# A mixture-of-experts layer: the first expert's turn on unsplit weights with 64 slots, and three more weight blocks loaded ahead

## Chip, cores and metric

The kernel runs on one core of one Trainium2 chip. The metric is device time in microseconds (us), the median of several executions; lower is better. Names of engines: PE (TensorE), DVE (VectorE), ACT (ScalarE), POOL (GpSimd), SP (SyncE, which issues nearly all loads of weights).

## What is computed

A trunk of two layers over 256 tokens of width 1024, all in float32. Each layer has a token mixer and a channel mixer; the channel mixer of the second layer is a mixture of 8 experts of which every token takes two:

```python
logits = h @ router
top_v, top_i = lax.top_k(logits, 2)
wts = softmax(top_v)
combine = sum(one_hot(top_i, 8) * wts)
for e in range(8):
    y = y + combine[..., e:e+1] * ((silu(h @ w1[e]) * (h @ w3[e])) @ w2[e])
```

with `w1`, `w3` of 1024 x 3584 and `w2` of 3584 x 1024. The router, worked out on the reference's own inputs, sends 60, 58, 49, 84, 77, 59, 69 and 56 tokens to experts 0 to 7.

## The kernel before

The change lies in `moe`, the second layer's experts, which is the last part of the program. All eight experts' weights pass once through the core as 336 blocks of 1024 KB, 42 of each expert: seven groups j of 512 hidden columns, in each two blocks of `w1`, two of `w3` and two of `w2`. The `w2` blocks of a group come after the `w1` and `w3` blocks of the next group, so that the first block of the second turn is the 41st of the stream, and that of the third turn the 83rd.

**Turns.** The experts are taken in eight turns. Expert 0 always has turn 0, so that its loads need no routing; the seven others are ordered by their number of tokens (`RANK`) and read by a register that SP loads once (`loads`, L1312). Expert 0 and the three fullest others take the "big" way, the four others the "small" one (`SMALL`), in turns that alternate: big, small, big, small and so on.

- A big turn has 128 slots. Each weight piece of 1024 columns is split into a rounded part `hi` (ACT, L1187) and the rest `lo` (DVE, L1188), and every tile of it costs three matmuls of 512 columns: L1408, L1409, L1410 for `w1` and `w3` (`up`), L1426 to L1428 for `w2` (`down`).
- A small turn has 64 slots (`CAP`). The float32 weights go to PE as they landed, as two half-width matmuls side by side (L1404 in `up`, L1423 in `down`), with no work on ACT and DVE for the weights.

The tokens of a turn are gathered by one-hot matmuls (`slots_of`, `gather`, L1377) into `xs` (small) or `xh`, `xl` (big); one gather serves a pair of turns (`GROUPS`). The results go back by `back` and `scatter`. If the count of tokens of an expert exceeds its slots (`excess`), a second part (`spill`) runs all experts again, twice.

**Loads.** `fetch` keeps the blocks on their way. At the start it issues as many as there are names in `FIRST`: 18, namely the places of two tiles that are needed only later (`acts`, `late`), fifteen `raw` buffers and `y`. After that only the `raw` names go round. SP issues loads strictly in order; a load waits for the release of its buffer, and for the load eight before it to have landed.

```python
live, blocks, expert = [], [], [0]
slots = list(FIRST)
```

A block's buffer is released in a big turn by DVE, when `lo` of its second piece is written, in a small turn by PE, after the block's last matmul. `hi` and `lo` have three buffers of 1024 columns each (`SPLIT_MOE`), six places of 512 KB. The order of instructions on PE, DVE, ACT and SP is that of the code: `pieces` yields one weight piece after another, and at each a clock ticks, on which the small steps hang (`after`, `SORT`, `BACK`).

Of the kernel before, what the change touches and what calls it, by code (L numbers as in the profile page):

```python
# [9 lines left out]
F32 = mybir.dt.float32  # L10
F32R = mybir.dt.float32r
# [3 lines left out]
ALU = mybir.AluOpType  # L15
# [3 lines left out]
P = 128  # L19
T = 256  # L20
D = 1024
KC = 8
# [5 lines left out]
NE = 8  # L28
# [29 lines left out]
NPRE = len(PRE)  # L58


RANK = [7, 0, 4, 1, 5, 2, 6, 3]
SMALL = [False, True] * 4
CAP = 64
NSMALL = sum(SMALL)
GROUPS = [(None, 0), (1, 2), (3, 4), (5, 6), (7, None)]


def constants():
# [14 lines left out]
    put("keyc", np.broadcast_to(np.array([1e6, 1, 2, 3, 4, 5, 6, 7])[None, :], (P, 8)))  # L83
    put("seq", np.broadcast_to(np.array(RANK)[None, :], (P, 8)))
    gmask = ((s <= t) & (i[:, None] // 64 == i[None, :] // 64)).astype(np.int32)
# [350 lines left out]
WOUT = ((2, 'BT'), (3, 'TT'))  # L436
MOE_BUFS = 15
PLACES = [f"raw{i}" for i in range(6)] + ["acts", "late"] + [f"raw{i}" for i in range(6, MOE_BUFS)]
FIRST = ["acts", "late"] + [f"raw{i}" for i in (6, 7, 8, 4, 5, 12, 13, 14, 9, 10, 11, 2, 3, 1, 0)] + ["y"]
PACE = (13, 9, 28)  # L440
PACED_FROM = 8
ARAW_BUFS = 2
# [4 lines left out]
SPLIT_MOE = 3  # L447
SUB = 1024
# [685 lines left out]
def moe(k, l, out):  # L1134
    tc, nc, A = k.tc, k.nc, k.A
    ctx = ExitStack()
    dp = ctx.enter_context(tc.tile_pool(name="moe", bufs=1, reuse_waits="tile"))
    sp = ctx.enter_context(tc.tile_pool(name="moew", bufs=1, reuse_waits="tile"))
# [12 lines left out]
    todo = [o + (h,) for o in order for h in range(2)]  # L1151
    live, blocks, expert = [], [], [0]

    once = {n: sp.tile([P, 2048], F32, name=n) for n in PLACES}
    once["y"] = dp.tile([P, 2048], F32, name="y")
    slots = list(FIRST)

# [18 lines left out]
    def prepare(eng=nc.vector):  # L1176

        block = blocks[0]
        w, at, _ = block
        q = len(part)  # L1180
        s = slice(q * SUB, (q + 1) * SUB)
        last = q == 2048 // SUB - 1
        if SMALL[at[0]]:
            ready.append((w[:, s], None, at + (q,), block if last else None))
        else:
            hi, lo = [sp.tile([P, SUB], F32R, name=n, bufs=SPLIT_MOE) for n in ("hi", "lo")]
            nc.scalar.activation(hi, w[:, s], AF.Copy)  # L1187
            eng.tensor_tensor(lo, w[:, s], hi.bitcast(F32), ALU.subtract)  # L1188
            ready.append((hi, lo, at + (q,), None))
        part.append(q)  # L1190
        if last:
            part.clear()
            blocks.pop(0)
            if not SMALL[at[0]]:
                done(block)
# [3 lines left out]
    def parts(n, kind=F32):  # L1199

        if n not in held:
            held[n] = sp.tile([P, 4, 512], kind, name=n)
        return held[n]

    turns = [0, 0]

    def room():
        turns[0] += 1
# [3 lines left out]
    ready = []  # L1212
    fetch(len(FIRST))

# [9 lines left out]
    n8, key, rank, more, idx = [S8[:, i] for i in range(5)]  # L1224
# [66 lines left out]
    def sort():  # L1291

        by = lambda a: a[:, None, :].to_broadcast([P, NE, NE])
        of = lambda a: a[:, :, None].to_broadcast([P, NE, NE])
        p, w = perm[:, 0], perm[:, 1]

        def ranks():
            nc.vector.scalar_tensor_tensor(key, n8, 8.0, k.k("keyc"), ALU.mult, ALU.add)
            nc.vector.tensor_tensor(w, of(key), by(key), ALU.is_gt)
            nc.vector.tensor_reduce(rank, w, AX.X, ALU.add)  # L1300
            nc.vector.tensor_tensor(p, by(rank), of(k.k("seq")), ALU.is_equal)
            nc.vector.tensor_tensor(w, p, by(iota[:, :NE]), ALU.mult)
            nc.vector.tensor_reduce(idx, w, AX.X, ALU.add)
            nc.vector.tensor_copy(idxi, idx)

        def turned(src, dst):
            for tt in range(2):
                nc.vector.tensor_tensor(w, p, by(src[:, tt]), ALU.mult)
                nc.vector.tensor_reduce(dst[:, tt], w, AX.X, ALU.add)

        def loads():
            _, v = nc.values_load_multi_w_load_instructions(idxi[0:1, 1:NE], engines=[mybir.EngineType.SP], min_val=0,  # L1312
                                                            max_val=NE - 1)
            expert.extend(v)

        def excess():
            nc.vector.tensor_scalar(more, rank, NSMALL - 0.5, float(P - CAP), ALU.is_le, ALU.mult)
            nc.vector.tensor_tensor(n8, n8, more, ALU.add)
            nc.vector.tensor_reduce(cnt, n8, AX.X, ALU.max)
            nc.vector.tensor_copy(cnti, cnt)  # L1320

        return [ranks, loads, lambda: turned(posm, posm_s), lambda: turned(comb, comb_s), excess]
# [13 lines left out]
    def slots_of(g):  # L1336

        Pm = dp.tile([P, 2, 2, P], F32R, name="Pm", bufs=2)
        for i, (t, io) in enumerate(zip(GROUPS[g], (iod, iota))):
            if t is not None:  # L1340
# [6 lines left out]
    def back(g, Pm, gs, PT):  # L1347
        pg = k.pg()
        here = [i for i in range(2) if GROUPS[g][i] is not None]
        for i in here:  # L1350
# [12 lines left out]

    def places(g):

        xs = dp.tile([P, KC, CAP], F32, name="xs") if GROUPS[g][0] is not None else None
        xl = [dp.tile([P, KC, P], F32R, name=n) for n in ("xh", "xl")] if GROUPS[g][1] is not None else None
        return xs, xl

# [28 lines left out]
    def up(e, j, b, p, x):  # L1398
        for o, hi, lo in pieces(e, j, b):
            for z in range(SUB // 512):  # L1400
                kc = o + z
                if SMALL[e]:
                    for n in range(2):
# [8 lines left out]
    def down(e, j, py, act):  # L1412
        if j == 0:
            py += [k.pc() for _ in range(1 if SMALL[e] else 2)]
        for o, hi, lo in pieces(e, j, 2):
            for n in range(2):
                for z in range(SUB // 1024):
                    c = o // 2 + z
                    s = slice(z * 1024 + n * 512, z * 1024 + n * 512 + 512)
                    first, last = j == 0 and c == 0, j == NJ - 1 and c == 3  # L1420
                    if SMALL[e]:
                        a = (c % 2) * P + (c // 2) * CAP
# [170 lines left out]
    for _ in range(PRESPLIT):  # L1593
        prepare()
    with tc.manual_schedule(engines=ORDERED | LOADS):
        y = choose()
        idle = k.pj()
        busy(IDLE[0])
        pp = place()
        busy(IDLE[1])  # L1600
        for c in range(3):
            rows_of(c, y)
        rows_of(0, y, True)
        nc.vector.tensor_tensor(posm, posm, pp[:, 0:2 * NE].rearrange("p (a b) -> p a b", a=2), ALU.add)
        new = slots_of(0)
        nc.vector.tensor_copy(n8, pp[:, 2 * NE:3 * NE])
        rows_of(1, y, True)
        rows_of(2, y, True)
        to = places(0)
        for kc in range(KC):  # L1610
            gather(0, new[1], kc, to, k.pj if kc % 4 > 1 else k.pg)
        weigh()
        after(BACK, lambda: back(*new))
        for n, f in enumerate(sort()):
            after(SORT + n, f)
        group = new, to
        for e in range(NE):
            i = 0 if SMALL[e] else 1
            if e and i == 0:
                group = nxt  # L1620
            (_, _, gs, PT), (xs, x2) = group
            for j in range(NJ):
                ph = [k.pj()]
                up(e, j, 0, ph[0], x2 if i else xs)
                act, steps = hidden(e, ph)
                delay = DELAY
                if (e, j) == (NE - 1, NJ - 1):
                    delay, last = LAST, gains()
                after(delay[0], steps[0])
                ph.append(k.pj())  # L1630
                up(e, j, 1, ph[1], x2 if i else xs)
                for d, f in zip(delay[1:], steps[1:]):
                    after(d, f)
                if i == 1 and e < NE - 1:
                    g = e // 2 + 1
                    if j == NJ - 2:
                        new = slots_of(g)
                        after(BACK, lambda: back(*new))
                    if j == NJ - 1:
                        nxt = new, places(g)  # L1640
                        for kc in range(KC):
                            after(kc * 2048 // SUB // 4, lambda kc=kc, g=g, n=nxt: gather(g, n[0][1], kc, n[1]))
                if pend:
                    down(*pend[:4])
                    if pend[4]:
                        for d, f in in_turn(pend[0], *scatter(pend[0], pend[2], *pend[4])):
                            after(d, f)
                if j == 0:
                    py = []
                pend = (e, j, py, act, (gs[:, i:i + 1], PT, i) if j == NJ - 1 else None)  # L1650
        while tasks:
            tick()
        down(*pend[:4])
        banks = iter((k.pg, k.pg, k.pj, k.pj))
        finish(scatter(pend[0], pend[2], *pend[4], lambda: next(banks)()), *last)
# [64 lines left out]
    n = nc.values_load(cnti[0:1, 0:1], min_val=0, max_val=T + P)  # L1720
# [103 lines left out]
```

## Time and profile before

| what | value |
|---|---|
| median of 3 runs | 1780.85 us (1779.85 to 1782.62) |
| the profiled execution | 1777.78 us, of which its span 1776.0 us |
| PE busy | 1703.6 us, 96% of the span |
| DVE, ACT busy | 1161.7 us (65%), 838.2 us (47%) |
| DMA | 520.92 MB, mean 293 GB/s |
| blocks of expert weights | 336 loads, 1024 KB each |

The profile gives, for any stretch, the busy time of each engine, the granted clock of PE (1.00 is 2.4 GHz, 0.50 is 1.2 GHz) and what the DMA engines moved; it lists instructions in order of time, and what each waited for. Busy shares of PE say little alone, since matmuls are pipelined and their ends are modelled.

### The profile page before, as it was taken

What the parts mean: (1) busy time and instruction counts of PE and PEld (TensorE: products, weight loads), DVE (VectorE), ACT (ScalarE), POOL (GpSimd) and SP (SyncE); (2) the same over time, 40 slices, a digit from 0 to 9 for tenths busy, and PEclk for the clock granted to TensorE, in tenths of its full rate; (3) what the DMA queues carried; (4) which work ended last, traced back from release to release, by engine and by line L of the source; (5) the groups of instructions that cost most, each with busy time, mean ns of one, the idle gap of its engine ahead of it and who ended that gap; (6) DMA issues with size and microseconds to landing.
All of it is one profiled execution on the core that took longest, in us unless ns stands there. A gap on an engine that the chain in (4) does not pass through costs nothing.

```text
span 1776.0 us, 30054 instructions
## 1 busy us (share of the span) xinstructions
PE 1703.6 (96%) x11915; PEld 1400.8 (79%) x11915; DVE 1161.7 (65%) x1783; ACT 838.2 (47%) x1214; POOL 50.3 (3%) x100
## 2 busy tenths in 40 slices
PE   7998989989999799999999999999999999999997
PEld 6987879989999688799977875688656876578754
DVE  3789577787876879466669950588407972289611
ACT  3653234454444743244547740477306771267501
POOL 0000010010100000000000000000000000000001
PEclk9999899999999899899989999999999999999999
DMA  9445257687874333225678989999999999999995
GB/s 347 158 165 190 73 182 259 249 287 304 314 267 145 110 129 119 73 96 190 261 307 311 366 314 421 421 421 421 418 420 421 421 421 416 421 421 421 420 421 214
DMA packets 79972, 520.92 MB, mean 293 GB/s; under 512 B 9520, under 2 KB 10160, under 8 KB 22352
## 3 DMA queue, kind: packets, MB, share of 16 engines
q1 hardware_dynamic: 67440, 476.14, 67.7%
q0 software_dynamic: 11232, 40.90, 6.7%
q8 instruction: 95, 1.56, 0.4%
q10 hardware_dynamic: 1152, 1.89, 0.3%
q14 instruction: 53, 0.43, 0.1%
HBM read 517.84 MB, written 1.05 MB: 292 GB/s over the span
## 4 chain that ended last, share of the span: by engine, by line
PE 76%; issue 8%; DMA 7%; DVE 6%; ACT 1%; POOL 0%; SPq 0%; ACTq 0%; POOLq 0%; DVEq 0%
PE pj L1404 11%; PE pj L392 7%; PE pj L393 7%; PE pj L394 7%; PE pc L1423 6%; PE pj L1408 5%; PE pj L1410 5%; PE pj L1409 5%; DMA araw<-wada 4%; PE pc L1426 3%; PE pc L1428 3%; PE pc L1427 3%; DMA raw<-moe 2%; PE pg L1453 1%; DVE lo L369 1%
## 5 line engine op out<-in xcount | busy, mean ns | idle before, releaser
L1188 DVE TENSOR_TENSOR lo<-raw,hi 128x1024 fp32r<-128x1024 f32 x330 | 396.1, 1223 | 85.0 <-ACT hi L1187 77.9
L1187 ACT ACTIVATE hi<-raw 128x1024 fp32r<-128x1024 f32 x330 | 347.5, 1059 | 128.1 <-PE pj L1409 80.0
L367 ACT ACTIVATE hi<-raw 128x1024 fp32r<-128x1024 f32 (+2 forms) x209 | 213.9, 1025 | 280.7 <-PE pj L393 207.6
L369 DVE TENSOR_TENSOR lo<-raw,hi 128x1024 fp32r<-128x1024 f32 (+2 forms) x209 | 246.5, 1181 | 77.5 <-ACT hi L367 73.9
L392 PE MATMUL pj<-hh,hi 128*128 128x256 f32 x992 | 289.9, 292 | 4.8 <-DVE t L418 3.4
L394 PE MATMUL pj<-hh,lo 128*128 128x256 f32 x992 | 285.9, 288 | 1.3 <-DVE lo L369 1.3
L393 PE MATMUL pj<-hl,hi 128*128 128x256 f32 x992 | 286.2, 289 | 0.0
L1404 PE MATMUL pj<-raw,xs 128*64 128x256 f32 x1792 | 201.4, 381 | 0.0
L392 PEld LDWEIGHTS pj<-hh,hi 128*128 128x128 f32 x992 | 191.2, 193 | 12.1 <-issue 4.8
L394 PEld LDWEIGHTS pj<-hh,lo 128*128 128x128 f32 x992 | 191.1, 193 | 2.5 <-DVE lo L369 1.8
L393 PEld LDWEIGHTS pj<-hl,hi 128*128 128x128 f32 x992 | 191.3, 193 | 2.2 <-issue 1.3
L1408 PE MATMUL pj<-hi,xh 128*128 128x512 f32 x448 | 181.3, 405 | 0.5 <-ACT hi L1187 0.5
L1410 PE MATMUL pj<-lo,xh 128*128 128x512 f32 x448 | 178.5, 398 | 2.0 <-DVE lo L1188 1.9
L1409 PE MATMUL pj<-hi,xl 128*128 128x512 f32 x448 | 177.7, 397 | 0.0
L1404 PEld LDWEIGHTS pj<-raw,xs 128*64 128x64 f32 x1792 | 125.8, 137 | 64.9 <-issue 4.7
L1448 DVE TENSOR_TENSOR late<-late,pj 128x512 f32<-128x512 f32 (+1 forms) x56 | 30.8, 550 | 207.6 <-PE pj L1404 201.0
L1410 PEld LDWEIGHTS pj<-lo,xh 128*128 128x128 f32 x448 | 84.5, 189 | 25.7 <-DVE lo L1188 5.4
L1423 PE MATMUL pc<-raw,as 128*64 128x512 f32 x448 | 102.2, 595 | 0.0
L1408 PEld LDWEIGHTS pj<-hi,xh 128*128 128x128 f32 x448 | 84.8, 189 | 21.2 <-ACT hi L1187 1.9
L1409 PEld LDWEIGHTS pj<-hi,xl 128*128 128x128 f32 x448 | 84.7, 189 | 18.7
L256 DVE SCALAR_TENSOR_TENSOR aacc<-araw,csg,aacc 128x1024 f32<-128x1024 f32 x70 | 89.6, 1280 | 8.0 <-DMA araw<-wada 7.5
L1426 PE MATMUL pc<-hi,acts 128*128 128x512 f32 x224 | 88.3, 394 | 0.0
(432 smaller groups left out, 2749.2 us busy)
## 6 DMA issues: line engine op xcount, KB each, us to landing
raw<-moe SPq DMA_DIRECT2D x333, 1024.0 KB, 18.6
raw<-win SPq DMA_DIRECT2D x43, 1024.0 KB, 5.0
araw<-wada POOLq DMA_DIRECT2D x78, 512.0 KB, 5.3
raw<-f SPq DMA_DIRECT2D x33, 1024.0 KB, 7.3
raw<-wv SPq DMA_DIRECT2D x8, 1024.0 KB, 4.8
raw<-wog SPq DMA_DIRECT2D x8, 1024.0 KB, 5.0
raw<-wad SPq DMA_DIRECT2D x6, 1024.0 KB, 7.1
raw<-wor SPq DMA_DIRECT2D x4, 1024.0 KB, 5.1
```

The lines of the kernel that those rows point to most:

```text
L367: nc.scalar.activation(hi[:, :w], src, AF.Copy)
L369: nc.vector.tensor_tensor(lo[:, :w], src, hi[:, :w].bitcast(F32), ALU.subtract)
L392: nc.tensor.matmul(o, hi[:, s], ah[:, kc, :], start=kc == 0, stop=False)
L393: nc.tensor.matmul(o, hi[:, s], al[:, kc, :], start=False, stop=False)
L394: nc.tensor.matmul(o, lo[:, s], ah[:, kc, :], start=False, stop=kc == nk - 1)
L1187: nc.scalar.activation(hi, w[:, s], AF.Copy)
L1188: eng.tensor_tensor(lo, w[:, s], hi.bitcast(F32), ALU.subtract)
L1404: nc.tensor.matmul(p[64 * n:64 * n + 64, :T], x[:, kc], hi[:, z * 512 + n * T:z * 512 + n * T + T], start=kc == 0, stop=kc == KC - 1)
L1408: nc.tensor.matmul(p, x[0][:, kc], hi[:, s], start=kc == 0, stop=False)
L1409: nc.tensor.matmul(p, x[1][:, kc], hi[:, s], start=False, stop=False)
L1410: nc.tensor.matmul(p, x[0][:, kc], lo[:, s], start=False, stop=kc == KC - 1)
L1423: nc.tensor.matmul(py[0][64 * n:64 * n + 64], act[:, a:a + CAP], hi[:, s], start=first, stop=last)
```

## The change

Turn 0 becomes a small one. `SMALL` is now small, small, big, small, big, small, big, small: expert 0 has 64 slots and unsplit weights, and the three fullest of the others stay big. `GROUPS[0]` gathers only `xs`, 64 columns; the `xs` of turn 1, gathered during turn 0, lies in the fourth quarter of `late`. The test for too many tokens adapts to the new table. The pairs `hi` and `lo` become one tile of 2048 columns, `hl0` to `hl2`; since these are not needed before turn 2, they carry the 19th to 21st block at the start.

```diff
-SMALL = [False, True] * 4
+SMALL = [True] + [True, False] * 3 + [True]
 CAP = 64
-NSMALL = sum(SMALL)
-GROUPS = [(None, 0), (1, 2), (3, 4), (5, 6), (7, None)]
+GROUPS = [(0, None), (1, 2), (3, 4), (5, 6), (7, None)]
...
-FIRST = ["acts", "late"] + [f"raw{i}" for i in (6, 7, 8, 4, 5, 12, 13, 14, 9, 10, 11, 2, 3, 1, 0)] + ["y"]
+FIRST = ["acts", "late"] + [f"raw{i}" for i in (6, 7, 8, 4, 5, 12, 13, 14, 9, 10, 11, 2, 3, 1, 0)] + ["y"] + [
+    f"hl{i}" for i in range(3)]
...
-    once = {n: sp.tile([P, 2048], F32, name=n) for n in PLACES}
+    once = {n: sp.tile([P, 2048], F32, name=n) for n in PLACES + [f"hl{i}" for i in range(SPLIT_MOE)]}
...
-            hi, lo = [sp.tile([P, SUB], F32R, name=n, bufs=SPLIT_MOE) for n in ("hi", "lo")]
+            hl = sp.tile([P, 2 * SUB], F32R, name=f"hl{turns[2] % SPLIT_MOE}")
+            turns[2] += 1
+            hi, lo = hl[:, :SUB], hl[:, SUB:]
...
-            nc.vector.tensor_scalar(more, rank, NSMALL - 0.5, float(P - CAP), ALU.is_le, ALU.mult)
+            nc.vector.tensor_scalar(more, rank, -5.0, None, ALU.add)
+            nc.vector.tensor_tensor(more, more, more, ALU.mult)
+            nc.vector.tensor_scalar(more, more, 2.0, float(P - CAP), ALU.is_ge, ALU.mult)
...
-        xs = dp.tile([P, KC, CAP], F32, name="xs") if GROUPS[g][0] is not None else None
+        xs = None
+        if g == 1:
+            xs = parts("late")[:, 3].rearrange("p (k n) -> p k n", k=KC)
+        elif GROUPS[g][0] is not None:
+            xs = dp.tile([P, KC, CAP], F32, name="xs")
...
-                if i == 1 and e < NE - 1:
+                if (i == 1 or e == 0) and e < NE - 1:
```

On SP, around the first loads of `moe`; DMAHW names stand for the load eight before, DVE and PE for the engine that releases the buffer. Before:

```order
L1163 DMA raw0_9796<-moe 128x2048 [waits DMAHW1_49]
L1163 DMA y_9813<-moe 128x2048 [waits DMAHW2_49]
L1163 DMA raw6_10042<-moe 128x2048 [waits DMAHW3_49,DVE_49]
L1163 DMA raw7_10074<-moe 128x2048 [waits DMAHW4_49,DVE_49]
L1312 TENSOR_LOAD idxi_9838 [waits DVE_49]
L1312 ISA x14
L1163 DMA raw8_10168<-moe 128x2048 [waits DMAHW5_49,DVE_49]
```

And now:

```order
L1164 DMA raw0_9796<-moe 128x2048 [waits DMAHW1_49]
L1164 DMA y_9816<-moe 128x2048 [waits DMAHW2_49]
L1164 DMA hl0_9813<-moe 128x2048 [waits DMAHW3_49]
L1164 DMA hl1_9814<-moe 128x2048 [waits DMAHW4_49]
L1164 DMA hl2_9815<-moe 128x2048 [waits DMAHW5_49]
L1315 TENSOR_LOAD idxi_9844 [waits DVE_49]
L1315 ISA x14
L1164 DMA raw6_10135<-moe 128x2048 [waits DMAHW6_49,PE_49]
```

Three loads that wait for no compute engine have come in ahead of the register load, and the first load that reuses a buffer stands behind it and waits for PE in place of DVE.

On DVE, at the start of `moe`, where the one-hot tile `Pm` for the first gather is made. Before:

```order
L1604 TENSOR_TENSOR R<-R,pj 128x16
L1188 TENSOR_TENSOR lo<-acts,hi 128x1024 x2
L1343 TENSOR_SCALAR Pm<-cst,R 128x128 x2
L1606 COPY S_9837<-pj 128x8
L1277 SCALAR_TENSOR_TENSOR tl<-pc,rsq,th 128x384
L1188 TENSOR_TENSOR lo<-late,hi 128x1024
```

And now:

```order
L1613 TENSOR_TENSOR R<-R,pj 128x16
L1348 TENSOR_SCALAR Pm<-iod,R 128x128 x2
L1615 COPY S_9843<-pj 128x8
L1280 SCALAR_TENSOR_TENSOR tl<-pc,rsq,th 128x384 x2
L1280 SCALAR_TENSOR_TENSOR tl<-ada,rsq,th 128x256
```

The two `lo` pieces that stood ahead of `Pm` are gone, as are all splits of turn 0.

On ACT, in turn 2, the first that is big in both kernels: the splits of `w1` pieces. Before:

```order
L1187 ACTIVATE hi_11635<-raw13_11474 128x1024 [waits DMAHW5_49,DVE_49,PE_49]
L1187 ACTIVATE hi_11645<-raw13_11474 128x1024 [waits DVE_49,PE_49]
L1187 ACTIVATE hi_11658<-raw14_11488 128x1024 [waits DMAHW6_49,DVE_49,PE_49]
L1187 ACTIVATE hi_11668<-raw14_11488 128x1024 [waits DVE_49,PE_49]
L1445 ACTIVATE late_10025<-pj_11611 128x512
```

And now:

```order
L1190 ACTIVATE hl2_11099<-raw14_10928 128x1024 [waits DMAHW1_49,DVE_49,PE_49]
L1190 ACTIVATE hl0_11104<-raw14_10928 128x1024 [waits DVE_49,PE_49]
L1190 ACTIVATE hl1_11121<-raw9_10934 128x1024 [waits DMAHW2_49,DVE_49,PE_49]
L1485 ACTIVATE ys_11119<-pc_10681,gs_10399 128x512 [waits PE_49]
L1190 ACTIVATE hl2_11131<-raw9_10934 128x1024 [waits DVE_49,PE_49]
```

The order is the same; the target is now a tile that holds the `lo` part too, so that a new `hi` waits for the last matmul that reads either part (the `lo` product) where it waited for the last that reads `hi`, one matmul earlier.

## Rows read from the trace of the kernel before

**Rows 1.** Stretches of 50 us: length, busy of PE, PEld, DVE, ACT, POOL, PEclk, DMA share, GB/s

```profile
900.00:950.00 50.00, 44.50 (x194) 35.14 (x194) 39.71 (x94) 30.77 (x42) 0.00 (x0) 0.90 0.87 357
950.00:1000.00 50.00, 50.00 (x224) 40.72 (x223) 45.35 (x42) 39.54 (x42) 0.00 (x0) 1.00 0.94 358
1000.00:1050.00 50.00, 48.69 (x266) 39.08 (x266) 37.09 (x45) 33.99 (x49) 0.00 (x0) 1.00 0.84 309
1050.00:1100.00 50.00, 50.00 (x366) 29.47 (x364) 10.44 (x18) 6.46 (x13) 0.00 (x0) 1.00 1.01 415
```

**Rows 2.** The same view for the rest of the experts' stage

```profile
1060.00:1750.00 690.00, 686.07 (x4002) 473.51 (x4000) 370.06 (x411) 319.89 (x399) 2.90 (x8) 1.00 1.01 420
...
1752.00:1754.00 2.00, 2.00 (x10) 0.69 (x10) 0.00 (x0) 0.38 (x1) 0.00 (x0) 1.00 0.24 98
```

**Rows 3.** Instructions of PE in order of time: starts of turns, last product

```profile
916.23 0.73 PE L1408 MATMUL pj<-hi,xh 128*128 128x512 f32 x1
...
1044.12 7.13 PE L1404 MATMUL pj<-raw,xs 128*64 128x256 f32 x64
...
1125.32 0.48 PE L1408 MATMUL pj<-hi,xh 128*128 128x512 f32 x1
...
1755.76 2.31 PE L1423 MATMUL pc<-raw,as 128*64 128x512 f32 x10
```

**Rows 4.** What SP's queue waited for from 909 to 1060 us: total, times, longest

```profile
SPq L1163 <- DVE lo L1188: 96.5, 33, 12.8
...
SPq L1312 <- DVE lo L1188: 7.9, 1, 7.9
```

**Rows 5.** SP's loads in order of time after the first seventeen

```profile
909.31 0.33 SPq L1163 DMA_DIRECT2D y<-moe  x1
924.60 0.33 SPq L1163 DMA_DIRECT2D raw<-moe  x1
...
938.07 0.81 SPq L1163 DMA_DIRECT2D raw<-moe  x2
```

**Rows 6.** DMA issues: the 18th block, KB, us from issue to landing

```profile
y<-moe SPq DMA_DIRECT2D x1, 1024.0 KB, 19.9
```

**Rows 7.** DVE and PE in order of time, at the first gather

```profile
906.66 2.35 DVE L1188 TENSOR_TENSOR lo<-acts,hi 128x1024 fp32r<-128x1024 f32 x2
...
909.35 0.49 PE L1377 MATMUL pg<-Pm,th 128*128 128x128 f32 x2 [1.79 <-DVE Pm L1343]
```

**Rows 8.** Stretches of 10 us, columns as in rows 1

```profile
910.00:920.00 10.00, 9.95 (x38) 8.99 (x38) 5.99 (x21) 4.20 (x10) 0.00 (x0) 0.50 1.01 422
920.00:930.00 10.00, 10.00 (x46) 7.84 (x45) 6.05 (x6) 6.98 (x8) 0.00 (x0) 1.00 1.02 422
```

**Rows 9.** PE in turn 7, a small one: four blocks of `up`, two of `down`

```profile
1700.12 7.13 PE L1404 MATMUL pj<-raw,xs 128*64 128x256 f32 x64
...
1707.08 3.60 PE L1423 MATMUL pc<-raw,as 128*64 128x512 f32 x16
```

**Rows 10.** DVE in order of time: the ranks' first and last step

```profile
932.78 0.16 DVE L1298 SCALAR_TENSOR_TENSOR S<-S,cst 128x8 f32<-128x8 f32 x1
...
934.27 0.17 DVE L1304 CAST idxi<-S 128x8 int32<-128x8 f32 x1
```

**Rows 11.** PE's groups from 916 to 1044 us: busy, mean ns, idle before (`tl` has as many)

```profile
L1377 PE MATMUL pg<-Pm,th 128*128 128x192 f32 x16 | 3.2, 283 | 0.6 <-DVE xl L1384 0.6
```

**Rows 12.** ACT, DVE and PE in order of time in turn 2, one piece

```profile
1168.72 1.06 ACT L1187 ACTIVATE hi<-raw 128x1024 fp32r<-128x1024 f32 x1 [0.34 <-PE pj L1409]
...
1169.81 1.23 DVE L1188 TENSOR_TENSOR lo<-raw,hi 128x1024 fp32r<-128x1024 f32 x1 [0.17 <-ACT hi L1187]
...
1171.79 0.39 PE L1409 MATMUL pj<-hi,xl 128*128 128x512 f32 x1
...
1172.02 0.40 PE L1410 MATMUL pj<-lo,xh 128*128 128x512 f32 x1
```

**Rows 13.** DVE in turn 2: a step that stands between the splits

```profile
1176.52 0.68 DVE L1448 TENSOR_TENSOR late<-late,pj 128x512 f32<-128x512 f32 x1
```

More of the change, by code (lines that the diff above doesn't have):

```diff
@@ L1203, in parts @@
         return held[n]
-    turns = [0, 0]
+    turns = [0, 0, 0]
     def room():
```

## The prediction

> **What bounds the kernel now.** I looked first at the stretches of 50 us, not at busy shares: PE is busy for 96% of the span, which would make it the bound and the change a plain saving of PE work. The column of the transfers says something else. From 1060 us on they move 420 GB/s without a break [rows 2]; that is the most that any longer stretch shows, so a block of 1024 KB (1.049 MB) costs 1.049 / 420 = 2.50 us of transfer, however early it is asked for. Before that, the same stream runs at 357, 358, 309 and 415 GB/s [rows 1]. Against 420 that lacks 63 + 62 + 111 + 5 = 241 GB/s in stretches of 50 us, or 241 x 50 / 420 = **28.7 us** of transfer time that is never won back, since the stream is full for all the rest.
>
> Why it lacks is in the waits of SP's queue: from 909 to 1060 us it stood 96.5 us behind `lo` of turn 0, DVE's release of a buffer, and 7.9 us before the register load [rows 4]. The 18th block was issued at 909.31 and landed 19.9 us later, at 929.2; the next loads went out at 924.60 and shortly after, and then none until 938.07 [rows 5, 6], so the queue ran dry after the second of them.
>
> PE has hardly more room. Turn 0 runs from 916.23 to 1044.12 (127.9 us), turn 1 to 1125.32 (81.2 us), and from there to the end of the last product at 1758.07 it takes 632.8 us [rows 3], 686.07 of 690 us busy [rows 2]. The last block lands at about 1753 [rows 2], 5 us before that product ends. So transfers and PE are matched to about 1% in the pairs of turns; what differs is turn 0, where one resource waits for the other.
>
> **The change, part by part.** *Loads.* The rows of SP show three new loads, each waiting only for the load eight before. `y` went out when the tenth block landed (909.31), so the three follow at steps of 2.50: 911.8, 914.3, 916.8, and land at 931.7, 934.2 and 936.7. The next load must go out before some 934 us for the stream to stay full. It now waits for two things. First PE: the third block must be used. PE begins earlier, since `Pm` no longer stands behind 2.35 us of `lo` and the first gather waited for `Pm` [rows 7], and that gather has half the columns. It took 916.23 - 909.35 = 6.9 us [rows 3, 7]; with half of it and the 2.35 us off, turn 0 would start at 910.4, and I take 912; at full clock a small block costs (7.13 + 3.60) / 6 = 1.79 us [rows 9], at half clock 3.58, so three blocks are used at 917 to 923. Second the register load, which follows on the ranks; these stand behind a copy that waits for PE after three blocks, take 1.7 us [rows 10], and the load after them came 938.07 - 934.44 = 3.6 us later [rows 5, 10]: 923 to 929. Either way the queue is still full, with 5 us to spare. After that, blocks are released every 1.8 us by PE and needed every 2.50 us: no load waits for a buffer until turn 2. The stream then has no hole: the 83rd block, the first of turn 2, lands at 929.2 + 65 x 2.50 = 1091.5, and the last, 318 blocks after `y`, at 1724, against some 1753 now. This term is **minus 28.7 us**; between nothing (all waits return in another form) and this value I take nearly all of it, because DVE's release, 96.5 us of the waits, no longer exists before turn 2.
>
> *PE.* Turn 0 now has 40 blocks of 1.79 us (72 us) before the first of turn 1, the gather for turns 1 and 2 of twice 3.2 us [rows 11], and up to 5 us for 10 us at half clock [rows 8]: from 912 to about 996, against 1044.12. Turn 1 adds its 81.2 us: PE would want the 83rd block at 1077 and gets it at 1091.5. So of some 45 us that PE saves, the last 15 are spent waiting, and turn 2 starts with the first split after that block (1.06 us on ACT [rows 12]) at 1092.6: 32.7 us earlier than 1125.32. From there PE needs its 632.8 us again.
>
> *Splits.* In three big turns a new `hi` now waits for the `lo` product. In the piece of [rows 12] ACT starts at 1168.72, `lo` is written by 1171.04 and needed at 1172.02: 0.98 us of room. One matmul later means 1172.02 - 1171.79 = 0.23 us less; a DVE step in between takes 0.68 us [rows 13]. That still fits, by 0.07 us, so a single delay costs nothing; where two meet (scatter, gather, starts of turns) PE may lose 0.23 us each. Bounds: none, and 3 turns x 84 pieces x 0.23 = 58 us if every piece paid. The row is nearest to none; I take 2 us. PE's own sum is then -32.7 + 2 = -30.7; that of the transfers, -28.7, is the smaller gain and decides.
>
> *Small things.* The longer test for too many tokens is two more operations on eight columns, 0.17 us each by the cast of [rows 10], on a DVE that has no splits left in turn 0: nothing. The `xs` of turn 1 in `late` uses a quarter that nothing else reads then: nothing. The tail after the last product is unchanged.
>
> Sum: 28.7 less a little for starts that don't fit exactly, **minus 28 us**. The profiled execution (1777.78) would become 1749.8; the median of the runs stands 3.1 us above it, so I predict **1752.9 us**.
>
> **A cold PE.** Turn 1 has something that this stage never had: PE waiting for weights. It needs 81.2 / 42 = 1.93 us a block there, its transfer 2.50, so that from 996 on it has caught up at about the 57th block (1027 us) and then waits some 0.6 us at each. PE was granted 1.2 GHz from 910 to 920 us, after it had stood for 1.79 us before `Pm`, and 2.4 GHz in the next ten, after work without a break [rows 7, 8]. At 1.2 GHz a small block takes 3.58 us, more than its transfer; PE would fall behind and be busy without a break, which is what brought the clock back. Such a spell loses some 5 us, and only what is missing at the 83rd block counts: a spell just there leaves a gain of 32.7 - 5 - 2 = 26 us. Were the clock low from the 57th block to the 83rd, 26 x 3.58 = 93 us would bring PE there at 1120, and 5 us of gain were left. I count on the row: a PE without a break gets its clock back. The Trainium skill ("TensorE: Matmul & The Clock Gate", section "HAM oscillation — how this bites in real kernels") warns of exactly such a loop, where each tile's work is shorter than the wait for the next weights and the clock drops at every tile; by that rule turn 1 would stay slow, and the sum would be the 5 us. No row here shows waits as short as 0.6 us that come again and again, so whether it holds for them is open.
>
> **Rivals.** (1) *Only the three blocks count.* The refills come as late as before for another reason (the register load, PE's start), and all that is won is 3 x 2.50 = 7.5 us: 1773. For it: 7.9 us of SP's wait were for the register. Against: its source now comes some 10 us earlier. 10%. It is also what would remain if the places `hl` were not free in time; the rows of SP speak against that, as they wait for no engine.
> (2) *PE is the only bound.* Then the 45 us pass in full: 1736. Against: 420 GB/s is never exceeded over a longer stretch. 5%.
> (3) *Part is lost again.* Short stalls in the split loop (a fifth of the pieces, 12 us) or repeated spells at half clock take 8 to 16 us of it: about 1764. For it: PE and transfers are matched, so that what PE loses from turn 2 on can't be won back. 12%.
> (4) *The split loop binds.* If the 0.98 us of room is used up (DVE steps behind each other in most groups), each of 252 pieces pays 0.23 us; -28 + 58 = 30 us slower, 1811. It decides against the change once more than half of the pieces pay. Against: the 0.07 us that remain after both delays. 3%.
> (5) *Expert 0 overflows.* With more than 64 tokens it would run the second part, twice 336 blocks more, 1678 us. It has 60 by the reference's inputs: 1%.
> (6) *The clock stays low in turn 1.* 5 us of gain less the 2 of the splits: 1778. For it: PE has never waited so regularly in this stage; against: the clock's return in [rows 8]. 3%.
>
> **The numbers.** The forecast has 66% and alone would be 1748 to 1759. With most of (3) the range is **1746 to 1768**; (1), (2) and (4) lie outside. A measurement here tells about 0.2% (3.6 us) from no change. Faster by more: 66 + 10 + 5 + nearly all of 12 = 92%; the same 4%, (6) above all; slower 4%.
>
> **What would show it.** Right: three loads between 911 and 917 us; no pause of SP's loads from 930 to 938; some 410 GB/s or more in each stretch of 50 us from 900 on; the first matmul of turn 0 near 912, of turn 1 near 996, of turn 2 near 1093; PE waiting for transfers late in turn 1; the last L1423 ending near 1729. Wrong: a gap in the loads after the 21st block (rival 1), turn 2 before 1085 (rival 2), PE waiting for `lo` by more than some us in turns 2, 4 and 6 (rivals 3, 4), or PE below full clock there.

## The result and the profile after

The changed kernel takes 1752.11 us (median of 4 runs, 1751.55 to 1758.41) against 1780.96 us: a ratio of 0.9845, 95% interval 0.9822 to 0.9869. The profiled execution took 1751.72 us, of which its span 1749.7. The prediction was 1752.9 us. The number and the course of the changed kernel came out; what the prediction said of the kernel **before** did not, and the experiments show it.

The stretches of the changed kernel, columns as in [rows 1]:

```profile
900.00:950.00 50.00, 48.89 (x367) 32.01 (x368) 15.24 (x74) 10.01 (x25) 0.00 (x0) 0.97 1.00 408
950.00:1000.00 50.00, 49.40 (x370) 27.98 (x368) 5.34 (x17) 7.83 (x25) 0.00 (x0) 1.00 1.01 420
1000.00:1050.00 50.00, 44.72 (x316) 22.34 (x311) 4.91 (x12) 3.27 (x8) 0.00 (x0) 1.00 1.01 421
1050.00:1100.00 50.00, 38.73 (x250) 19.83 (x249) 5.98 (x7) 7.39 (x11) 0.00 (x0) 1.00 1.01 421
1100.00:1400.00 300.00, 298.05 (x1574) 215.26 (x1574) 198.92 (x211) 169.91 (x200) 0.00 (x0) 1.00 1.01 421
...
1724.00:1726.00 2.00, 2.00 (x12) 0.54 (x8) 0.42 (x1) 0.00 (x0) 0.00 (x0) 1.00 0.47 197
1726.00:1728.00 2.00, 2.00 (x12) 0.77 (x12) 0.00 (x0) 0.39 (x1) 0.00 (x0) 1.00 0.03 12
```

Transfers run at 408 to 421 GB/s from 900 us on, where [rows 1] had 309 to 358 up to 1050. The price stands in the column of PE, the first behind the length: from 950 to 1100 us it is idle for 0.6 + 5.3 + 11.3 = 17.2 us. PE's instructions in order of time say for whom it waits (start, duration, idle before and releaser):

```profile
912.57 3.17 PE L1413 MATMUL pj<-acts,xs 128*64 128x256 f32 x16
...
994.85 7.13 PE L1413 MATMUL pj<-raw,late 128*64 128x256 f32 x64
...
1071.44 1.95 PE L1413 MATMUL pj<-raw,late 128*64 128x256 f32 x16 [0.44 <-DMA raw<-moe]
1074.02 1.94 PE L1432 MATMUL pc<-raw,as 128*64 128x512 f32 x8 [0.63 <-DMA raw<-moe]
...
1094.97 0.50 PE L1417 MATMUL pj<-hl,xh 128*128 128x512 f32 x1 [1.26 <-ACT hl L1190]
...
1726.09 5.37 PE L1432 MATMUL pc<-raw,as 128*64 128x512 f32 x24
```

Turn 0 starts at 912.57, turn 1 at 994.85, turn 2 at 1094.97; the last product ends at 1726.09 + 5.37 = 1731.46 [rows 3: 916.23, 1044.12, 1125.32, 1758.07]. So 49.3 us are saved by the start of turn 1, 30.4 are left at turn 2, 26.6 at the last product. Late in turn 1 each block of 1.95 us of work waits for its transfer. From 1100 to 1400 PE is busy 298.05 of 300 us: PE is the bound again there, with the transfers close behind. The list of PE's waits from 909 us to the end (total, times, longest) agrees:

```profile
PE pj L1413 <- DMA raw<-moe: 9.3, 18, 1.7
PE pc L1432 <- DMA raw<-moe: 5.4, 10, 0.6
...
PE pj L1417 <- ACT hl L1190: 1.3, 1, 1.3
...
PE pj L1419 <- DVE hl L1191: 0.5, 1, 0.5
```

The 14.7 us of waits for transfers all lie before turn 2.

SP's loads in order of time, and what its queue waited for from 909 to 1060 us:

```profile
910.93 0.33 SPq L1164 DMA_DIRECT2D y<-moe  x1
913.41 5.29 SPq L1164 DMA_DIRECT2D hl<-moe  x3
925.58 23.07 SPq L1164 DMA_DIRECT2D raw<-moe  x12
```

```profile
SPq L1164 <- DMA raw<-moe: 106.6, 53, 3.0
...
SPq L1315 <- DVE R L1312: 4.9, 1, 4.9
```

The three new loads go out from 913.4, the refills from 925.6, after the register load; there is no pause from 930 to 938. The 96.5 us behind DVE's `lo` [rows 4] are gone; apart from the register load SP waits almost only for its own earlier loads (1.2 us in all for PE's releases).

### The profile page after: what moved, and what is told of

It reads as the page before. It is cut to its first block, busy times and chain, and to the rows that moved or that the text cites. A ratio compares the mean times of both kernels' runs of the same rounds, so it can differ in the third digit from the quotient of the medians.

```text
span 1749.7 us, 29708 instructions
## 1 busy us (share of the span) xinstructions
PE 1666.1 (95%) x11957; PEld 1343.5 (77%) x11957; DVE 1054.8 (60%) x1684; ACT 749.3 (43%) x1129; POOL 50.5 (3%) x100
## 4 chain that ended last, share of the span: by engine, by line
PE 79%; DVE 10%; DMA 7%; ACT 2%; issue 1%; SPq 0%; DVEq 0%; ACTq 0%
PE pj L1413 11%; PE pj L392 8%; PE pj L393 8%; PE pj L394 8%; DMA raw<-moe 6%; PE pc L1432 6%; PE pj L1419 4%; PE pj L1417 4%; PE pj L1418 4%; DVE lo L369 2%; PE pc L1435 2%; PE pc L1437 2%; PE pc L1436 2%; PE pg L1462 1%; DVE ff L752 1%
## 5 line engine op out<-in xcount | busy, mean ns | idle before, releaser
L1191 DVE TENSOR_TENSOR hl<-raw,hl 128x1024 fp32r<-128x1024 f32 x252 | 303.2, 1223 | 74.3 <-ACT hl L1190 68.4
L1190 ACT ACTIVATE hl<-raw 128x1024 fp32r<-128x1024 f32 x252 | 265.7, 1060 | 114.8 <-PE pj L1419 61.1
L1457 DVE TENSOR_TENSOR late<-late,pj 128x256 f32<-128x256 f32 (+1 forms) x56 | 29.0, 517 | 280.4 <-PE pj L1413 274.5
L1417 PE MATMUL pj<-hl,xh 128*128 128x512 f32 x336 | 135.4, 403 | 1.3 <-ACT hl L1190 1.3
L1419 PE MATMUL pj<-hl,xh 128*128 128x512 f32 x336 | 133.2, 396 | 0.6 <-DVE hl L1191 0.5
L1418 PE MATMUL pj<-hl,xl 128*128 128x512 f32 x336 | 132.7, 395 | 0.0
L1432 PE MATMUL pc<-raw,as 128*64 128x512 f32 x552 | 127.4, 596 | 5.4 <-DMA raw<-moe 5.4
L1465 ACT ACTIVATE as<-pg 128x256 f32<-128x256 f32 x35 | 13.4, 382 | 207.2 <-PE pg L1462 207.2
L1432 PEld LDWEIGHTS pc<-raw,as 128*64 128x64 f32 x552 | 38.1, 137 | 70.3 <-issue 58.4
L392 PE MATMUL pj<-BK,hi 128*128 128x256 f32 (+1 forms) x280 | 80.8, 294 | 0.9 <-ACT BK L994 0.9
L393 PE MATMUL pj<-vt,hi 128*128 128x256 f32 (+1 forms) x280 | 80.8, 293 | 0.1
```

Of the source, the lines that this page charges most:

```text
L392: nc.tensor.matmul(o, hi[:, s], ah[:, kc, :], start=kc == 0, stop=False)
L393: nc.tensor.matmul(o, hi[:, s], al[:, kc, :], start=False, stop=False)
L1417: nc.tensor.matmul(p, x[0][:, kc], hi[:, s], start=kc == 0, stop=False)
L1418: nc.tensor.matmul(p, x[1][:, kc], hi[:, s], start=False, stop=False)
L1419: nc.tensor.matmul(p, x[0][:, kc], lo[:, s], start=False, stop=kc == KC - 1)
L1432: nc.tensor.matmul(py[0][64 * n:64 * n + 64], act[:, a:a + CAP], hi[:, s], start=first, stop=last)
```

## The experiments

Two of the numbers of the changed kernel needed a test: what the three extra blocks and the joint tile are worth, and which resource sets the end of either kernel.

**The changed kernel once more**, beside the next three. 

> The changed kernel once more, as the measure for the other three of this group. 1752 us, give or take 1; all theories agree.

 Measured: 1752.85 us, 5 runs.

**18 blocks on their way.**

```diff
-FIRST = [...] + ["y"] + [f"hl{i}" for i in range(3)]
+FIRST = [...] + ["y"]
```

> The changed kernel without the three loads into the buffers of rounded weights: 18 blocks on their way, as before. Theory (the stream has no hole because PE releases the buffers of turn 0 early): the first refill still goes out near 925.6 us, before the 18th block has landed (about 931), so the stream stays full and the time is 0 to 2 us over that of the changed kernel: 1752 to 1754. Rival (the three blocks are the gain): three transfers of 2.50 us come later, 1759.6 us, and the stretch from 900 to 950 us falls from 408 to about 345 GB/s.

 Measured: 1751.36 us (1749.69 to 1754.89; ratio to the kernel before 0.9841, 0.9821 to 0.9860), no different from the 1752.85. The first refill goes out even earlier than the 925.6 expected, at 919.23, while `y` of 912.33 is still under way, and the stretch from 900 to 950 falls from 408 to 398 GB/s, not to the rival's 345 (SP's loads, then the stretch):

```profile
912.33 0.33 SPq L1163 DMA_DIRECT2D y<-moe  x1
919.23 20.80 SPq L1163 DMA_DIRECT2D raw<-moe  x11
```

```profile
900.00:950.00 50.00, 48.89 (x383) 32.72 (x383) 15.40 (x74) 10.02 (x25) 0.00 (x0) 1.00 0.97 398
```

The three blocks, which name the change, are worth nothing that can be measured here. Rival 1 falls.

**18 blocks, hi and lo in tiles of their own.**

```diff
-            hl = sp.tile([P, 2 * SUB], F32R, name=f"hl{turns[2] % SPLIT_MOE}")
-            turns[2] += 1
-            hi, lo = hl[:, :SUB], hl[:, SUB:]
+            hi, lo = [sp.tile([P, SUB], F32R, name=n, bufs=SPLIT_MOE) for n in ("hi", "lo")]
```

> 18 blocks on their way, and rounded parts in tiles of their own as before (ACT's next hi no longer waits for the last lo product): what is left of the change is expert 0's first turn on unsplit weights. Theory: from turn 2 to the end of the span the changed kernel took 636.5 us and the kernel before 632.75, and the joint tile is the difference; since the last block lands at 1726 and the last product can't end much before 1729, of these 3.7 us 1 to 3.7 come back: 1748 to 1751 us if the 18 alone cost nothing. If the joint tile costs nothing: no difference to the run with 18 and the joint tile. The PE waits for ACT's hi and DVE's lo in turns 2, 4 and 6 show which.

 Measured: 1749.85 us (1748.20 to 1752.66; ratio 0.9833, 0.9814 to 0.9852). By medians that is 1.5 us under ahead_18, and the intervals overlap. The profiled executions show the size better. PE's first product of turn 2 and its last product in ahead_18, then in this kernel:

```profile
1096.32 0.50 PE L1416 MATMUL pj<-hl,xh 128*128 128x512 f32 x1 [1.26 <-ACT hl L1189]
...
1727.35 5.37 PE L1431 MATMUL pc<-raw,as 128*64 128x512 f32 x24
```

```profile
1095.50 0.50 PE L1414 MATMUL pj<-hi,xh 128*128 128x512 f32 x1 [1.28 <-ACT hi L1187]
...
1724.24 5.37 PE L1429 MATMUL pc<-raw,as 128*64 128x512 f32 x24
```

From the start of turn 2 to the end of the last product the joint tile takes 636.4 us, the separate tiles 634.1: 2.3 us. These are single executions, but the others agree: the changed kernel, changed_again, ahead_18 and early_21 show 636.3 to 637.1 with the joint tile, ahead_18_apart, pairs_21 and early_pairs_21 634.1 to 635.1 without.

**21 blocks, tiles of their own** (three more blocks as pairs of 512 KB loads).

```diff
+            if n[:2] == "hl":
+                w = [once.pop(m + n[2:]) for m in ("hi", "lo")]
+                for i, t in enumerate(w):
+                    nc.sync.dma_start(t, A["moe"][expert[e], j, b][:, h * 2048 + i * SUB:h * 2048 + (i + 1) * SUB])
```

> 21 blocks on their way as in the changed kernel, but the rounded parts in tiles of their own: each of the three extra blocks goes as two loads of 512 KB, one into a hi tile, one into a lo tile. Theory: as 18 blocks with tiles of their own, give or take 1 us: 1748 to 1751. Rival (the three blocks are the gain): 7.5 us faster than 18 blocks with tiles of their own.

 Measured: 1750.75 us (1748.82 to 1756.75; ratio 0.9842, 0.9821 to 0.9863), the same as with 18.

**Two products in place of three** in turns 2, 4 and 6.

```diff
-                nc.tensor.matmul(p, x[1][:, kc], hi[:, s], start=False, stop=False)
...
-                    nc.tensor.matmul(py[n], al[:, c], hi[:, s], start=False, stop=False)
```

> The changed kernel with two products in place of three in turns 2, 4 and 6 (the product of the weights' high part with the tokens' low part is left out), so that PE has a third less to do there, some 43 us in each. Theory (transfers and PE are matched, and no block can come earlier): the last block lands at 1726 as before and the last product ends some 2 to 3 us after it, in place of 5.4: 1747 to 1751 us; PE's work drops by some 125 us and its waits for transfers grow by as much. Rival (PE alone is the bound): 1751 - 125 = 1626 us.

 Measured: 1749.96 us (1749.58 to 1754.29; ratio 0.9831, 0.9809 to 0.9854), where PE alone would have given 1626. The stretch from 1100 to 1400 us and the last product:

```profile
1100.00:1400.00 300.00, 272.56 (x1320) 159.95 (x1318) 200.93 (x218) 172.43 (x208) 0.00 (x0) 1.00 1.01 421
```

```profile
1727.89 1.94 PE L1431 MATMUL pc<-raw,as 128*64 128x512 f32 x8 [0.45 <-DMA raw<-moe]
```

PE now waits for transfers to the very last block (0.45 us), and ends at 1729.8. The stream runs at 406 to 421 GB/s without a break up to 1722 us and still ends at about 1726. That is the floor which the transfers set: the changed kernel, at 1731.5, stands some 2 us above it. One part of the expectation did not come: PE's waits for transfers did not grow by 125 us. From 1094 to 1732 us its busy time falls by 51 us (630.9 to 579.9), and of its waits there 16.6 us are for transfers and 27.7 us for the split parts `hl` in the big turns.

**Half of turn 1's transfers.**

```diff
+            n_cols = 1024 if e == 1 else 2048
-            nc.sync.dma_start(w, A["moe"][expert[e], j, b][:, h * 2048:(h + 1) * 2048])
+            nc.sync.dma_start(w[:, :n_cols], A["moe"][expert[e], j, b][:, h * 2048:h * 2048 + n_cols])
-            ready.append((w[:, s], None, ...
+            ready.append((w[:, :SUB] if at[0] == 1 else w[:, s], None, ...
```

> The changed kernel with half of turn 1's transfers: each of its 42 blocks loads its first 1024 columns alone and PE uses these twice, so that PE does the same work and 21 x 2.50 = 52.5 us of transfer are gone. Theory (the saving of turn 0 beyond the gain is waited away before turn 2, and from there PE needs its 636 us whatever comes): turn 1 takes PE's own 81.2 us from 994.9, turn 2 starts at 1076 to 1078 in place of 1095, and the time is 17 to 19 us shorter, 1733 to 1735. Rival a (transfers alone are the bound): 52 us shorter, 1700. Rival b (PE alone, no loss in turn 1): unchanged, 1752.

 Measured: 1727.07 us (1722.94 to 1730.89; ratio 0.9689, 0.9661 to 0.9717). This kernel leaves out half of turn 1's weights. The gain is more than the 17 to 19 expected: 25.8 us by the medians (changed_again was run in another group), 22.1 by the spans of the profiled executions (1749.9 to 1727.8). Of PE, the first products of turns 1 and 2 and the last of all:

```profile
996.15 7.13 PE L1414 MATMUL pj<-raw,late 128*64 128x256 f32 x64
...
1074.44 0.48 PE L1418 MATMUL pj<-hl,xh 128*128 128x512 f32 x1
...
1704.67 5.37 PE L1433 MATMUL pc<-raw,as 128*64 128x512 f32 x24
```

Turn 2 starts without a wait, 21.5 us before the 1095.9 of changed_again, and the last product ends 1710.04 - 1074.44 = 635.6 us later, nearly as there (636.3). So turn 1 of the changed kernel holds some 20 us of PE's time that only transfers take, and from turn 2 on PE has no more to give: neither rival fits. The expectation was too small because it gave turn 1 the 81.2 us of the kernel before; without waits it takes 1074.44 - 996.15 = 78.3. Turn 1 of the kernel before also holds the last products on `hi` and `lo` (24) and the scatter of a big turn 0; here both are those of a small one.

**The kernel before with the joint tile.** The edit is the part of ahead_18_apart's diff that is shown, the other way round. 

> The kernel before with nothing changed but the tiles of the rounded parts: hi and lo of a piece in one tile of 2048 columns, three of them. Theory: with 18 blocks ahead the joint tile cost 636.4 - 634.1 = 2.3 us from turn 2 to the last product, in three turns with splits; here there are four: 3 us slower, 2 to 5 (1783 to 1786). Rival (each piece pays 0.23 us): 4 x 84 x 0.23 = 77 us slower. Other rival (it costs nothing): 1781.

 Measured: 1782.09 us, 10 runs (1779.51 to 1790.80; ratio 1.0016, 1.0000 to 1.0032). That is 1.7 us more than the 1780.43 beside it, a little less than the 2 to 5 expected, at the edge of what can be told. From the start of turn 1 to the end of the last product its trace has 716.8 us, against the 713.95 of the kernel before: 2.9 us over three big turns. The rival's 77 us, every piece paying as in rival 4 of the prediction, are out of the question.

**The kernel before with 15 blocks.**

```diff
-FIRST = ["acts", "late"] + [...] + ["y"]
+FIRST = [...]
```

> The kernel before with 15 blocks on their way in place of 18 (acts, late and y are not loaded into). Theory: in the kernel before the stream has its hole whatever was loaded ahead, so that three blocks fewer put its end 3 x 2.50 = 7.5 us later, of which up to 3 us are covered by the 5 us that its last product ended after its last block: 4.5 to 7.5 us slower, 1785 to 1788. It is the reverse of what rival 1 gave the three blocks, and shows that they are worth something only where there is a hole. Rival (PE alone is the bound): unchanged, 1781.

 Measured: 1780.28 us, 10 runs (ratio 1.0001, 0.9988 to 1.0014). No change: the theory as it stood then **failed**, by its whole 4.5 to 7.5 us. From 930 to 940 us, the kernel before, then this one:

```profile
930.00:940.00 10.00, 8.02 (x34) 5.45 (x34) 9.12 (x20) 6.61 (x7) 0.00 (x0) 1.00 0.34 116
```

```profile
930.00:940.00 10.00, 8.02 (x34) 5.41 (x33) 8.10 (x17) 7.47 (x8) 0.00 (x0) 1.00 0.85 355
```

What was not loaded ahead is loaded in the pause. A refill waits for the release of the block 15 or 16 before it, whatever was loaded first, so the pause is a sign that all buffers are full. New theory: before the change PE alone sets the end, and the hole in the transfers costs nothing.

**The kernel before with half of turn 1's transfers.** The edit of half_loads on the kernel before. 

> The kernel before with half of turn 1's transfers: each of its 42 blocks loads its first 1024 columns alone and PE uses these twice; 21 x 2.50 = 52.5 us of transfer are gone, PE's work is the same. New theory (in the kernel before PE alone sets the end, its buffers are full at the end of turn 0, and the hole in the transfers is only the sign of full buffers): no change, 1779 to 1782 us. First theory (the hole is lost transfer time that sets the end): with 52.5 us of transfer less the 28.7 us come back, 1752 to 1775.

 Measured: 1779.61 us, 10 runs (ratio 0.9999, 0.9983 to 1.0014). Like half_loads it leaves out half of turn 1's weights. With 52.5 us of transfer gone nothing changes. Its stretches from 1000 to 1100 us, then PE's start of turn 1 and last product:

```profile
1000.00:1050.00 50.00, 48.68 (x236) 40.06 (x235) 41.41 (x48) 36.94 (x51) 0.00 (x0) 1.00 0.63 204
1050.00:1100.00 50.00, 50.00 (x361) 29.45 (x362) 12.19 (x20) 8.46 (x15) 0.00 (x0) 1.00 0.70 232
```

```profile
1051.04 7.13 PE L1405 MATMUL pj<-raw,xs 128*64 128x256 f32 x64
...
1759.50 5.37 PE L1424 MATMUL pc<-raw,as 128*64 128x512 f32 x24
```

PE's busy times are those of [rows 1] (48.69 and 50.00) with half the transfers. From the start of turn 1 to the end of the last product PE took 1764.87 - 1051.04 = 713.83 us here and 1758.07 - 1044.12 = 713.95 us in [rows 3]. The first theory, that the hole is lost time which sets the end, is refuted.

**Earlier loads.** If transfers bind the changed kernel up to turn 2, then what they lose earlier counts there. In the layer before, they stand still from 888 to 901 us, because the eighth load waits for PE to release its buffer (SP's queue stands 24.3 us for it), while six others are free. In the lines on `FIRST`, the list of the raw buffers is cut. A second edit goes with it: the experts are put in order 16 pieces later (`SORT`), which moves the register load back.

```diff
-... (6, 7, 8, 4, 5, 12, 13, 14, 9, 10, 11, 2, 3, 1, 0)] + ["y"] + [f"hl{i}" for i in range(3)]
+... (6, 7, 8, 4, 5, 2, 3)] + ["y"] + [f"hl{i}" for i in range(3)] + [... (1, 11, 0, 9, 10, 12, 13, 14)]
-SORT = 8
+SORT = 24
```

> The changed kernel with its first loads in another order: the buffers that are free during the layer before (raw2, raw3, y and the three of the rounded parts) are loaded as the 8th to 13th block, the ones that wait for PE there come last; and the order of the experts is worked out 16 pieces later, so that the register load no longer stands ahead of the first refills. In the changed kernel transfers stood from about 888 to 901 us (213 GB/s from 885 to 890, 0 from 890 to 900, 288 from 900 to 905: 14 us at 420). Theory (in the changed kernel the stream is the bound up to turn 2 and PE's spare time there is some 20 us): the stream runs without a break from 870 us, turn 2 starts 11 to 14 us earlier, near 1082, and the time is 11 to 14 us shorter: 1738 to 1741. Rival (PE is the bound, or what the stream gains is lost again in full buffers): 1751 to 1753.

 Measured: 1741.56 us (1738.05 to 1743.52, 5 runs; ratio to the kernel before 0.9775, 0.9751 to 0.9800), 11.3 us under the 1752.85 of changed_again, which ran in another group, within the 11 to 14 expected (the time itself was put at 1738 to 1741). The stretch from 890 to 900 in the changed kernel, then in this one, and this one's turn 2 and last product:

```profile
890.00:900.00 10.00, 10.00 (x87) 10.00 (x86) 4.18 (x15) 1.04 (x3) 0.00 (x0) 1.00 0.00 0
```

```profile
890.00:900.00 10.00, 10.00 (x86) 10.00 (x86) 4.65 (x15) 2.10 (x4) 0.00 (x0) 1.00 1.02 423
...
940.00:950.00 10.00, 10.00 (x76) 5.30 (x74) 0.42 (x1) 0.77 (x2) 0.00 (x0) 1.00 0.85 303
```

```profile
1084.30 0.50 PE L1417 MATMUL pj<-hl,xh 128*128 128x512 f32 x1 [1.26 <-ACT hl L1190]
...
1716.03 5.37 PE L1432 MATMUL pc<-raw,as 128*64 128x512 f32 x24
```

Turn 2 starts 11.6 us earlier than the 1095.9 of changed_again. Of the 14 us won, (420 - 303) x 10 / 420 = 2.8 go again from 940 to 950, after SP had waited for PE to release its first blocks. What each of the two edits gives was not tried apart.

**The same with tiles of their own.** 

> As early_21, with hi and lo in tiles of their own as in pairs_21. Theory: 2 us less than early_21, 1736 to 1739. Rival: 1749 to 1752.

 Measured: 1740.03 us (1736.17 to 1742.29; ratio 0.9769, 0.9744 to 0.9794). 1.5 us under early_21, less than the 2 expected, within its spread, and 1 us above the range expected. These two are the fastest of the kernels that load all weights.

## Why the prediction was right, and where it was not

*What bounds the kernel.* This step failed for the kernel before. The prediction put the end down to the transfers: "28.7 us of transfer time that is never won back". before_half took away 52.5 us of transfer and before_15 three blocks of lead, and nothing moved. Before the change PE is the bound throughout the experts' stage; SP's 96.5 us behind `lo` were full buffers, not lost time. The trace of the kernel before says so by itself. These are all of PE's waits from 909 us to the end:

```profile
PE pg L1360 <- DVE gs L1355: 3.1, 4, 1.1
PE pj L1410 <- DVE lo L1188: 1.9, 4, 0.8
PE pg L1377 <- DVE xl L1384: 1.8, 3, 0.6
PE pg L1377 <- DVE Pm L1343: 1.8, 1, 1.8
PE pg L1488 <- ACT ys L1476: 0.8, 1, 0.8
PE pj L1408 <- ACT hi L1187: 0.5, 1, 0.5
```

None is for a transfer; even if those for `hi` and `lo` stood behind one, they are 2.4 us in all.

*Why the number came out all the same.* The working set two limits beside each other and took the smaller gain: PE could end some 45 us earlier, the stream, if it never paused, could deliver its last block at 1724. That second limit needs no hole, only the first block's time, 420 GB/s and no wait for buffers, and it is the one that binds the changed kernel up to turn 2 (half_loads, two_products). It holds to some 2 us: transfers end at about 1726 in place of 1724. So the gain isn't the closed hole; it is PE's saving of turn 0, cut down by the transfers. That the hole's 28.7 us gave nearly the same number is luck of this kernel: before the change PE's last product ended only 5 us after the last block landed (1758 and 1753), so that it hardly mattered from which of the two ends the gain was counted. That the median came within 0.8 us is luck in part as well: the prediction of 1749.8 for a profiled execution met 1751.72, and the median stood 0.4 us above that, not the 3.1 that were added. The gain is 26.1 us by the profiled executions, 28.9 by these medians and 27.7 by those of changed_again and its group.

*PE.* The "some 45 us" that PE saves are 48 by the prediction's own starts of turn 1 (1044.12 - 996); 49.3 came. Predicted 912, 996 and 1092.6 for turns 0 to 2; 912.57, 994.85 and 1094.97 came. Of the last difference, 1.6 us are a later start of the stage (`y` goes out at 910.93, not 909.31). The waits ahead of turn 2 were put at 15 us; the list shows 14.7 for transfers and 1.3 for ACT. They cost more: by the 78.3 us of half_loads turn 1 lasts 1094.97 - 994.85 - 78.3 = 21.8 us longer than PE needs. The list falls short of that because the profile counts 1.95 us busy for a block with a wait before it, where four blocks without one take 7.13; the prediction's 15 falls short because turn 1's own work was taken 3 us too long and turn 2 started later.

*Splits.* Predicted 2 us for the joint tile; ahead_18 and ahead_18_apart give 2.3. From turn 2 to the last product the changed kernel takes 3.7 us more than the kernel before (636.5 against 632.75). Of the 1.4 us that the tile doesn't explain, 0.5 are the wait for DVE right after turn 2's first products (the 1.26 us for ACT stand before the 1094.97 and don't count here); half_loads, whose turn 2 starts without a wait, takes 635.6, 0.9 us less. The rest is open and within the spread of these traces.

*The clock.* PE's regular waits of 0.26 to 0.64 us late in turn 1, and one of 1.66, left the granted clock of the changed kernel at 1.00 (2.4 GHz) in every stretch of 5 us from 930 to 1725 us. The Trainium skill ("TensorE: Matmul & The Clock Gate", section "HAM oscillation — how this bites in real kernels") describes a loop in which each tile's work is shorter than the wait for the next weights and the clock drops at every tile. The prediction called turn 1 exactly such a loop, but 1.95 us of work stand against these waits there, and the trace of the changed kernel shows no drop; the gain of only 5 us, which the prediction set down to that rule, did not come.

*The rivals.* Rival 1 (only the blocks count) was built on the same mistake as the first step: ahead_18 shows its 7.5 us to be zero. Rival 2 (PE alone) is true of the kernel before, and of the changed one only from turn 2 on. Rivals 3 and 4 did not come: PE's waits for split parts behind the first piece of turn 2 are the 0.5 us of the list above. Nor did 5 and 6.

## What to carry to other kernels

A pause in a stream of loads is a loss only if its consumer ever waits for that stream: look for waits on transfers at the consumer before pricing the pause, and where there are none, read it as full buffers. Price a saving by the schedule of each resource to the point where they meet, and take the later one; that gave the right time here even with a wrong account of the kernel before. Once transfers bind, look upstream for where they stand still: the order of the first loads, with the sorting moved back, gave 11 us more, while three more blocks in flight gave nothing.

## What was unexpected

The clock fell where it had not been looked for. In pairs_21 it did so twice. Late in turn 1 PE waited 0.26 to 0.64 us before each block at full clock and then 2.17 us for one; busy without a break after that, it was granted 0.74 on average from 1055 to 1060 us. At the start of turn 2 it waited 1.31 us for ACT and, two products later, 0.52 us for DVE, and was granted 0.66 for 5 us. Both times 1.00 came back (a product and stretches of pairs_21):

```profile
1052.91 5.45 PE L1421 MATMUL pj<-raw,late 128*64 128x256 f32 x32 [2.17 <-DMA raw<-moe]
```

```profile
1050.00:1055.00 5.00, 2.83 (x24) 1.60 (x20) 0.00 (x0) 0.39 (x1) 0.00 (x0) 0.92 1.02 419
1055.00:1060.00 5.00, 5.00 (x26) 2.12 (x24) 0.42 (x1) 0.00 (x0) 0.00 (x0) 0.74 1.01 419
...
1090.00:1095.00 5.00, 3.08 (x13) 1.02 (x13) 1.32 (x2) 2.01 (x2) 0.00 (x0) 1.00 1.02 423
1095.00:1100.00 5.00, 5.00 (x15) 3.97 (x16) 3.49 (x3) 3.46 (x4) 0.00 (x0) 0.66 1.02 423
1100.00:1105.00 5.00, 5.00 (x23) 4.00 (x22) 4.47 (x4) 3.67 (x4) 0.00 (x0) 1.00 1.01 416
```

In two_products it fell as well, to 0.79 and 0.87 in the 10 us from 1095 and to 0.50 from 1545 to 1550. The changed kernel, changed_again, ahead_18 and ahead_18_apart have the same waits at the start of turn 2, and 1.66 to 1.82 us where pairs_21 has 2.17, and show 1.00 in every stretch of 5 us from 930 to 1110. What decides between them was not tried. In pairs_21 it costs little: the first drop lies in a turn where PE waits for transfers anyway, and from turn 2 to the last product it takes 1728.80 - 1093.70 = 635.1 us, ahead_18_apart 634.1.
